# Projecting the memory keys by token, as the values are, in a hybrid decoder block on one core

## The chip, the cores and the metric

The kernel runs on one core of one Trainium2 chip. The metric is the device time of one execution in microseconds (us). Three runs of the kernel before the change are shown, and one more execution was profiled.

## What is computed

One layer of a decoder trunk with three groups of heads, and a final RMSNorm. The sequence has 1024 tokens of 2048 features, the memory 256 tokens. The change lies in group C, cross-attention into the memory: the memory is normalised per token, projected to keys and values by one matrix of 2 x 512 columns, and each of the 1024 queries attends over the 256 keys in 4 heads of 128.

```python
  h = RMSNorm(x)
  P = h @ W_in                       # one input projection for all groups
  # group A: chunked gMLP gating; group B: gated DeltaNet, 8 heads
  m = rmsnorm(mem, mem_norm_g)       # 256 x 2048
  mk, mv = split(m @ w_mem_kv)       # 256 x 512 each, 4 heads x 128
  scores = einsum('bshd,bmhd->bhsm', cq, mk) * 128 ** -0.5
  out_c = softmax(scores) @ mv * silu(c_z)
  x = x + concat(A, B, C) @ W_out
y = RMSNorm(x)
```

## The kernel before

**Arithmetic.** Every large product is made of three matmuls in fp32r: each operand is split into a high and a low part (`split_to`: a copy that rounds on ACT, then a subtraction on DVE), and `triple` issues high x high, high x low and low x high into one PSUM bank. The products of x with W_in and with W_out are arranged as seven products instead of eight, with sums and differences of blocks.

**Order.** The code doesn't issue instructions as it reads. It records them in a `Plan`; `Plan.issue` then simulates all engines with a price for each instruction and each transfer, takes at every moment the ready instruction of the smallest rank and the earliest place in the code, and so writes out a fixed order for each engine's queue. Ranks are given by `rank(...)`; matmuls of products have rank 9, so work with a smaller rank goes between them as soon as it is planned to be ready. On the chip each engine follows its order and waits for what isn't there.

**Memory projection (the first 70 us).** Sixteen steps `k`, one for each 128 of the 2048 features. A step loads 128 rows of the 2 x 512 columns of `w_mem_kv`, scales them by the norm's weights (`gcol`) and splits them into `hi` and `lo`. The memory itself is transposed once (`spread_mem`) into `mh` and `ml`, features on partitions and tokens in columns. Values are accumulated by token: the memory (128 features x 128 tokens) is the stationary operand and the 512 columns of the weights move, into two banks `va[0]`, `va[1]`, which are the first two of the four `dn` banks. Keys are accumulated by feature: 128 columns of the weights, one head, are stationary and the 256 tokens move, into the first 256 columns of the four `acc` banks (`ka`). That form leaves keys with features on partitions, as the scores need them. Since the memory's norm factor belongs to a token, for the values it is a factor for each partition, but for the keys one for each column: at step 7 the two factor columns `rm` are put on a diagonal (`dg`), a product with ones spreads them to all partitions, and ACT copies the result to `rmb`.

Between the steps, `prep` normalises, transposes and splits the first token tiles of x, in two spare `dn` banks. For the first two token tiles (`tt < H0`) the products for the decays (`decay_rows`) go into columns 256 to 383 of `acc[0]` and `acc[1]` (`first_ab`), and ACT copies them out into `sums0`.

After the last step DVE multiplies each head's keys by `rmb` into halves of the two `et` tiles, ACT scales the values, and POOL stores both to DRAM (`kv_d`). The first product of the main part (`first_product(2, ...)`) follows on TensorE in six banks, the four `acc` and the first two `dn`.

**Attention.** Near the end of the scans of group B, POOL reads keys and values back, two heads at a time, into tiles of the rings `gt` (keys) and `inv` (values); a split gives `mkT` and `mv`. `attend` then works on one head at a time with banks from the ring of the four `dn` banks (`dnr()` gives the next). The scans of group B use the first two of the same banks (`scan_banks`) and `work` the others.

Of the kernel before, what the change touches and what calls it, by code (L numbers as in the profile page):

```python
# [9 lines left out]
F32 = mybir.dt.float32  # L10
F32R = mybir.dt.float32r
AF = mybir.ActivationFunctionType
ALU = mybir.AluOpType
# [4 lines left out]
P = 128  # L18
D = 2048
KT = D // P  # L20
# [4 lines left out]
NMEM = 256  # L25
GW, DW, XW = 512, 1024, 512
NG, NH, NX = 4, 8, 4
# [33 lines left out]
class Plan:  # L61
# [27 lines left out]
    @contextmanager  # L89
    def rank(self, cls):  # L90
        old, self.cls = self.cls, cls
        yield
        self.cls = old

    @contextmanager
    def behind(self, op):
        old, self.gate = self.gate, op
        yield
        self.gate = old
# [204 lines left out]
def kernel(  # L304
# [21 lines left out]
    x, mem, w_in, out = x[0], mem[0], w_in[0], out[0]  # L326
# [7 lines left out]
    V, S, G, PE, Q = R.dve, R.act, R.pool, R.pe, R.sp  # L334
    rank, behind = R.rank, R.behind

    def C(shape, name, dt=F32):
        return sb.tile(list(shape), dt, name=name, tag=name)[:]

    def DT(shape, name, dt=F32):  # L340
        return dr.tile(list(shape), dt, name=name, tag=name)[:]
# [41 lines left out]
    def tok(ap):  # L383

        return ap.rearrange("p (t c) -> p t c", c=P)
# [14 lines left out]
    et = [C([P, HT], f"et{i}") for i in range(2)]  # L400
    ring = {t: Slots(t, 2, [P, HT]) for t in ("kT", "qT", "vs", "kd", "ai")}
# [10 lines left out]
    rm = [rms[:, i : i + 1] for i in range(2)]  # L412
# [5 lines left out]
    dnr = Ring("dn", 4, [P, HT], pool=ps)  # L418
# [6 lines left out]
    ident, ones, utri = (C([P, P], n) for n in ("ident", "ones", "utri"))  # L425
# [11 lines left out]
    def split_to(hi, lo, src, eng):  # L437
        S.copy(hi, src)
        eng.tensor_tensor(out=lo, in0=src, in1=hi, op=ALU.subtract)

    def mm(a, lhs, rhs, start, stop, cls=9):
        with rank(cls):
            return PE.matmul(a, lhs, rhs, start=start, stop=stop, skip_group_check=True)

    def triple(a, l, r, start, stop, cls=9):

        mm(a, l[0], r[0], start, False, cls)
        mm(a, l[0], r[1], False, False, cls)
        return mm(a, l[1], r[0], False, stop, cls)
# [31 lines left out]
    def rows_of(d, q, tt):  # L481
        return d[2 * q : 2 * q + 2, :, tt * 2 * P : (tt + 1) * 2 * P].rearrange("j p n -> p j n")

    def twos_of(t):
        return t.rearrange("p (j n) -> p j n", j=2)
# [11 lines left out]
    def kv_parts(k):  # L497
        n = XW if k == 0 else 2 * XW
        return [slice(i, i + n) for i in range(0, 2 * XW, n)]

    def load_kv(k):
        for i, sl in enumerate(kv_parts(k)[::-1]):
            (S if (k, i) == (0, 0) else Q).dma_start(kvraw[k % 4][:, sl], w_mem_kv[k * P : (k + 1) * P, sl])
# [22 lines left out]
    va, ka = dnr.bufs[0:2], acc  # L526
    flip = dnr.bufs[2:4]

    def spare():
        turn["dn"] = 1 - turn["dn"]  # L530
        return flip[turn["dn"]]
# [8 lines left out]
    pt = acc[3]  # L540
# [4 lines left out]
    def times_g(o, tp, q):  # L545
        V.tensor_tensor(out=o, in0=tp, in1=bc(gcol[:, 16 + 4 * q : 20 + 4 * q], P), op=ALU.mult)

    def spread_mem(q):
        h, l = (ring[t](F32R).rearrange("p (k n) -> p k n", k=4) for t in ("gt", "inv"))
        for mt in range(2):  # L550
            tp = spare()
            for k in range(4):
                PE.transpose(tp[:, k * P : (k + 1) * P], mem_rows[mt][q][:, k * P : (k + 1) * P], ident)
            sl = slice(mt * P, (mt + 1) * P)
            with rank(2):
                split_to(h[:, :, sl], l[:, :, sl], tok(tp), V)
        return h, l
# [15 lines left out]
    H0 = NT // 2  # L573

    def first_ab(tt):
        return ka[tt][:, NMEM : NMEM + P]

    def decay_rows(a, q, t, start):

        with R.together():  # L580
            for j in range(4):
                k = 4 * q + j
                PE.matmul(a[j * 32 : (j + 1) * 32], abw[:, k * 16 : k * 16 + 32], t[:, j],
                          start=start, stop=q == NQ - 1, skip_group_check=True)

    def put0(tt):
        def put(q, tp):
            t = tok(ring["tn"]())
            with rank(1):
                times_g(t, tp, q)  # L590
            with rank(2):
                split_to(ahq[q][:, tt], alq[q][:, tt], t, V)
            if tt < H0:
                decay_rows(first_ab(tt), q, t, False)
            with rank(5):
                Q.dma_start(rows_of(h0_d, q, tt), twos_of(t.rearrange("p k c -> p (k c)")))

        return put
# [8 lines left out]
    for k in range(KT):  # L607
        mh, ml = mhl[k // 4]
        if k >= 4:
            with rank(3):  # L610
                load_kv(k)
        hi, lo = kvhi[k % 2], kvlo[k % 2]
        with rank(2):
            for sl in kv_parts(k)[::-1]:
                raw = kvraw[k % 4][:, sl]
                if k == 0:
                    V.tensor_scalar(hi[:, sl], raw, gcol[:, k : k + 1], None, op0=ALU.mult)
                else:
                    S.activation(hi[:, sl], raw, AF.Copy, scale=gcol[:, k : k + 1])
                V.scalar_tensor_tensor(lo[:, sl], raw, gcol[:, k : k + 1], hi[:, sl], op0=ALU.mult, op1=ALU.subtract)  # L620
        kk = k % 4
        for mt in range(2):
            sl = slice(mt * P, (mt + 1) * P)
            triple(va[mt], (mh[:, kk, sl], ml[:, kk, sl]), (hi[:, XW:], lo[:, XW:]), k == 0, k == KT - 1)
        for h in range(NX):
            sl = slice(h * P, (h + 1) * P)
            triple(ka[h][:, :NMEM], (hi[:, sl], lo[:, sl]), (mh[:, kk], ml[:, kk]), k == 0, False)
        kvmark.append(R.ops[-1])
        if k == 0:
            with behind(kvmark[-1]), rank(2):  # L630
                G.dma_start(abw[:, 0 : KT * 16].rearrange("p (k c) -> p k c", c=16),
                            w_in[:, C_AB : C_AB + 16].rearrange("(k p) c -> p k c", p=P))
        if k in (1, 4, 8):
            with behind(kvmark[-1]):
                mhl.append(spread_mem(len(mhl)))
        if k == 1:
            load_x(0, "vs", kvmark[1:2] * 4)
        if k == 3:
            for mt in range(2):
                V.tensor_copy(rm[mt], row_scale(mem_rows[mt]))  # L640
        if k == 4:
            load_x(1, "kd", kvmark[4:5] * 4)
        if k == 5:
            prep(0, put0(0), spare)
        if k == 7:

            dg, rmb = (ring["E"]()[:, 0:NMEM] for _ in range(2))
            for mt in range(2):
                V.tensor_scalar(dg[:, mt * P : (mt + 1) * P], ident, rm[mt], None, op0=ALU.mult)
            pt = spare()  # L650
            PE.matmul(pt[:, 0:NMEM], ones, dg, start=True, stop=True)
            S.copy(rmb, pt[:, 0:NMEM])
        if k == 9:
            prep(1, put0(1), spare)
            load_x(2, "kT", (kvmark[6], kvmark[7], kvmark[7], kvmark[8]))
        if k == 13:
            load_x(3, "qT", (kvmark[10], kvmark[11], kvmark[11], kvmark[12]))
            with rank(2):
                prep(2, put0(2), spare, (2, 3, 0, 1))

    kv_d = DT([2, NX, P, NMEM], "kvd")
    with rank(1):
        kfs = [t[:, i * NMEM : (i + 1) * NMEM] for t in et for i in range(2)]
        for h in range(NX):
            V.tensor_tensor(out=kfs[h], in0=ka[h][:, :NMEM], in1=rmb, op=ALU.mult)
    for h in range(NX):
        with rank(2.5):
            G.dma_start(kv_d[0, h], kfs[h])
    for mt in range(2):
        t = ring[("ai", "kd")[mt]]()  # L670
        with rank(1):
            S.activation(t, va[mt], AF.Copy, scale=rm[mt])
        with rank(2.5):
            G.dma_start(kv_d[1, :, :, mt * P : (mt + 1) * P].rearrange("h p e -> p h e"), tok(t))
    with rank(2):
        prep(3, put0(3), spare, (2, 3, 0, 1))
    sums0 = ring["xr"].bufs[1][:, 0:HT]
# [15 lines left out]
    with rank(3.5):  # L693
        S.activation(nal, nal, AF.Exp)
        V.tensor_scalar(nal, nal, -1.0, None, op0=ALU.mult)
        pt = dnr.bufs[3]
# [1029 lines left out]
    for n, (tag, to) in enumerate((("gt", mkT), ("inv", mv))):  # L1726
        for i in range(NX // 2):
            t = ring[tag](F32R).rearrange("p (h s m) -> p h s m", h=2, s=2)
            G.dma_start(t[:, :, 1].bitcast(F32), kv_d[n, 2 * i : 2 * i + 2].rearrange("h p m -> p h m"))
            with rank(1.5):  # L1730
                split_to(t[:, :, 0], t[:, :, 1], t[:, :, 1].bitcast(F32), V)
            to += [t[:, 0], t[:, 1]]
    xab = [heir(b, f"xa{i}", f"ut{i}", 2 * HT, F32R) for i, b in enumerate(ring["ut"].bufs)]
    xat = [t[:, i * HT : (i + 1) * HT] for t in xab for i in range(2)]
# [186 lines left out]
```

## Time and profile before

| | |
|---|---|
| runs before | 1587.89, 1590.94, 1589.88 us; median 1589.88 |
| the profiled execution | 1590.5 us; its span from the first to the last instruction 1588.7 us |
| granted TensorE clock, mean | 0.998 |
| TensorE (PE) busy | 1575.6 us, 99% of the span |
| VectorE (DVE), ScalarE (ACT), GpSimd (POOL) busy | 1287.4, 1016.2, 311.7 us |
| moved by DMA | 425.77 MB, mean 268 GB/s |

Nearly all instructions are issued from one line (300, where the plan issues them), so rows of the profile are told apart by tile names: `dn<-wlo,gt` writes a `dn` bank from the tiles wlo and gt. In the memory projection `gt` and `inv` hold the memory's high and low parts (`mh`, `ml`), `whi` and `wlo` the weights' (`hi`, `lo`). In rows of the timeline the first number is the start, the second the duration (of all that are merged, with their count behind x), and brackets give the idle time of the engine before it. PE rows are matmuls and transposes, PEld loads of the stationary operand; both overlap their neighbours, and their ends are modelled, so a pace is read from start to start.

### The profile page before, as it was taken

To read this page: it belongs to the slowest core of one execution; us is meant where nothing else is said; L and a number is where in the kernel's file an instruction comes from. 1 tells how busy PE (TensorE), PEld (TensorE's weight loads), DVE (VectorE), ACT (ScalarE), POOL (GpSimd) and SP (SyncE) were. 2 spreads that over 40 slices of the span, in tenths; PEclk is the share of its full clock that TensorE was granted. 3 is DMA by queue.
4 is the path that set the end of the run, shared out by engine and by line. 5 is a ranking of instruction groups with operands and counts; after the bars stand their busy time and mean duration, and the time that the engine had idled before them with its cause. 6 is when DMAs were issued, how large, how long until landed. Compare 5 with 4: busy or idle time off the path is not lost.

```text
span 1588.7 us, 25645 instructions
## 1 busy us (share of the span) xinstructions
PE 1575.6 (99%) x8762; PEld 1317.2 (83%) x8762; DVE 1287.4 (81%) x1961; ACT 1016.2 (64%) x2088; POOL 311.7 (20%) x513
## 2 busy tenths in 40 slices
PE   9999999999999999999999999999999999999997
PEld 8878888888888888888888888888888888888886
DVE  5868996989899998997988776777768788688775
ACT  6762685776656788866775667766566864344355
POOL 1200042332402424235343133121000000000001
PEclk9999999999999999999999999999999999999999
DMA  8988868988679868986779775798877779688646
GB/s 305 319 279 278 274 214 306 349 303 268 199 253 345 270 215 283 357 306 219 263 233 356 240 259 188 242 327 257 283 255 260 260 238 355 198 283 294 202 146 238
DMA packets 213219, 425.77 MB, mean 268 GB/s; under 512 B 23112, under 2 KB 58672, under 8 KB 213088
## 3 DMA queue, kind: packets, MB, share of 16 engines
q1 hardware_dynamic: 190464, 367.40, 68.9%
q0 software_dynamic: 21840, 55.40, 10.5%
q8 instruction: 69, 1.13, 0.3%
q10 hardware_dynamic: 784, 1.33, 0.2%
q14 instruction: 62, 0.51, 0.1%
HBM read 335.40 MB, written 88.11 MB: 267 GB/s over the span
## 4 chain that ended last, share of the span: by engine, by line
PE 98%; DMA 1%; DVE 0%; issue 0%; ACTq 0%; ACT 0%; POOLq 0%; POOL 0%; DVEq 0%
PE acc L300 69%; PE dn L300 29%; DMA wraw<-in_w_in_dram 0%; DMA wraw<-in_w_mem_kv_dram 0%; DVE alo L300 0%; DVE zl L300 0%; ACTq L300 0%; ACT y2w L300 0%; DVE tn L300 0%; DVE kd L300 0%; DVE vs L300 0%; DVE inv L300 0%; POOLq L1916 0%; POOL small L300 0%; DVE whi L300 0%
## 5 line engine op out<-in xcount | busy, mean ns | idle before, releaser
L300 PE MATMUL acc<-ahi,whi 128*128 128x512 f32 (+1 forms) x1328 | 455.6, 392 | 0.0
L300 PE MATMUL acc<-ahi,wlo 128*128 128x512 f32 (+1 forms) x904 | 355.0, 393 | 0.0
L300 PEld LDWEIGHTS acc<-ahi,whi 128*128 128x128 f32 x1328 | 247.8, 188 | 47.7
L300 ACT CAST ahi<-raws 128x1024 fp32r<-128x1024 f32 x141 | 147.9, 1049 | 86.7 <-PE dn L300 40.4
L300 PEld LDWEIGHTS acc<-ahi,wlo 128*128 128x128 f32 x904 | 170.0, 188 | 32.6 <-issue 0.2
L300 PE MATMUL acc<-alo,whi 128*128 128x512 f32 (+1 forms) x480 | 187.5, 391 | 0.0
L300 PE MATMUL acc<-ahi,zh 128*128 128x512 f32 x424 | 167.2, 394 | 0.0
L300 PE MATMUL acc<-ahi,zl 128*128 128x512 f32 x424 | 167.2, 394 | 0.0
L300 PE MATMUL acc<-alo,zh 128*128 128x512 f32 x424 | 167.1, 394 | 0.0
L300 ACT CAST whi<-wraw 128x1024 fp32r<-128x1024 f32 (+1 forms) x78 | 80.6, 1033 | 70.4 <-PE acc L300 42.8
L300 DVE TENSOR_TENSOR wlo<-wraw,whi 128x1024 fp32r<-128x1024 f32 (+1 forms) x78 | 93.6, 1200 | 25.5 <-ACT whi L300 22.0
L300 POOL TENSOR_TENSOR small<-small,mhalf 128x1 f32<-128x1 f32 x26 | 16.6, 643 | 491.1 <-DVE small L300 488.9
L300 DVE TENSOR_TENSOR alo<-raws,ahi 128x1024 fp32r<-128x1024 f32 x71 | 87.5, 1233 | 21.9 <-ACT ahi L300 21.7
L300 PEld LDWEIGHTS acc<-alo,whi 128*128 128x128 f32 x480 | 90.3, 188 | 17.4
L300 DVE TENSOR_TENSOR ahi<-raws,ahi 128x1024 fp32r<-128x1024 f32 x70 | 85.4, 1220 | 18.8 <-ACT ahi L300 17.3
L300 DVE TENSOR_TENSOR alo<-y,ahi 128x1024 fp32r<-128x1024 f32 x65 | 79.3, 1220 | 17.4 <-ACT ahi L300 17.1
L300 PEld LDWEIGHTS acc<-ahi,zl 128*128 128x128 f32 x424 | 79.7, 188 | 15.3
L300 PEld LDWEIGHTS acc<-ahi,zh 128*128 128x128 f32 x424 | 79.8, 188 | 15.3
L300 PEld LDWEIGHTS acc<-alo,zh 128*128 128x128 f32 x424 | 79.7, 188 | 15.2
L300 ACT CAST ahi<-y 128x1024 fp32r<-128x1024 f32 x65 | 68.2, 1049 | 37.3 <-PE dn L300 17.6
L300 PE MATMUL dn<-whi,ahi 128*128 128x512 f32 x232 | 77.6, 389 | 0.0
L300 PE MATMUL acc<-whi,ahi 128*128 128x512 f32 x216 | 73.6, 392 | 0.0
(582 smaller groups left out, 3744.8 us busy)
## 6 DMA issues: line engine op xcount, KB each, us to landing
wraw<-in_w_in_dram SPq DMA_DIRECT2D x80, 512.0 KB, 5.1
raws<-sa SPq DMA_DIRECT2D x61, 512.0 KB, 5.3
y<-in_w_in_dram SPq DMA_DIRECT2D x40, 512.0 KB, 5.2
wraw<-in_w_out_dram SPq DMA_DIRECT2D x32, 512.0 KB, 4.9
raws<-h0d SPq DMA_DIRECT2D x29, 512.0 KB, 6.0
y<-sa SPq DMA_DIRECT2D x27, 512.0 KB, 4.8
raws<-sd SPq DMA_DIRECT2D x42, 256.0 KB, 2.9
raws<-hTd SPq DMA_DIRECT2D x16, 512.0 KB, 5.2
```

Of the source, the lines that this page charges most:

```text
L300: o.fn(*o.args, **o.kw)
```

## The change

Keys are now accumulated like the values: the memory is stationary, the 512 key columns of the weights move, and `acc[0]`, `acc[1]` take the two token tiles. The decay products of the first two token tiles move to `acc[2]`, `acc[3]`, and their first matmul starts the bank's sum. The norm factor is then one for each partition, so the diagonal, its product and the copy at step 7 go, and DVE scales two tiles of 128 x 512 in place of four of 128 x 256. POOL stores them to `key_d` in two transfers, by token. Where attention begins the keys are read back by token, 256 columns (two heads) at a time, four transposes turn them in a `dn` bank, and the split reads that bank.

```diff
     def first_ab(tt):
-        return ka[tt][:, NMEM : NMEM + P]
+        return ka[2 + tt][:, 0:P]
...
             if tt < H0:
-                decay_rows(first_ab(tt), q, t, False)
+                decay_rows(first_ab(tt), q, t, q == 0)
...
-        for h in range(NX):
-            sl = slice(h * P, (h + 1) * P)
-            triple(ka[h][:, :NMEM], (hi[:, sl], lo[:, sl]), (mh[:, kk], ml[:, kk]), k == 0, False)
+        for mt in range(2):
+            sl = slice(mt * P, (mt + 1) * P)
+            triple(ka[mt], (mh[:, kk, sl], ml[:, kk, sl]), (hi[:, 0:XW], lo[:, 0:XW]), k == 0, k == KT - 1)
...
-        if k == 7:
-
-            dg, rmb = (ring["E"]()[:, 0:NMEM] for _ in range(2))
-            for mt in range(2):
-                V.tensor_scalar(dg[:, mt * P : (mt + 1) * P], ident, rm[mt], None, op0=ALU.mult)
-            pt = spare()
-            PE.matmul(pt[:, 0:NMEM], ones, dg, start=True, stop=True)
-            S.copy(rmb, pt[:, 0:NMEM])
...
-    kv_d = DT([2, NX, P, NMEM], "kvd")
-    with rank(1):
-        kfs = [t[:, i * NMEM : (i + 1) * NMEM] for t in et for i in range(2)]
-        for h in range(NX):
-            V.tensor_tensor(out=kfs[h], in0=ka[h][:, :NMEM], in1=rmb, op=ALU.mult)
-    for h in range(NX):
+    kv_d = DT([NX, P, NMEM], "kvd")
+    key_d = DT([2, P, XW], "keyd")
+    for mt in range(2):
+        with rank(1):
+            V.tensor_scalar(et[mt], ka[mt], rm[mt], None, op0=ALU.mult)
         with rank(2.5):
-            G.dma_start(kv_d[0, h], kfs[h])
+            G.dma_start(key_d[mt], et[mt])
...
             t = ring[tag](F32R).rearrange("p (h s m) -> p h s m", h=2, s=2)
-            G.dma_start(t[:, :, 1].bitcast(F32), kv_d[n, 2 * i : 2 * i + 2].rearrange("h p m -> p h m"))
+            raw = t[:, :, 1].bitcast(F32)
+            if n == 0:
+                G.dma_start(raw, key_d[:, :, i * NMEM : (i + 1) * NMEM].rearrange("t p c -> p t c"))
+                d = dnr()
+                with rank(1.5):
+                    for h in range(2):
+                        for m in range(2):
+                            PE.transpose(d[:, (2 * h + m) * P : (2 * h + m + 1) * P], raw[:, m, h * P : (h + 1) * P], ident)
+                src = d.rearrange("p (h m) -> p h m", h=2)
+            else:
+                G.dma_start(raw, kv_d[2 * i : 2 * i + 2].rearrange("h p m -> p h m"))
+                src = raw
             with rank(1.5):
-                split_to(t[:, :, 0], t[:, :, 1], t[:, :, 1].bitcast(F32), V)
+                split_to(t[:, :, 0], t[:, :, 1], src, V)
```

More of the change, by code (lines that the diff above doesn't have):

```diff
@@ L673 @@
         with rank(2.5):
-            G.dma_start(kv_d[1, :, :, mt * P : (mt + 1) * P].rearrange("h p e -> p h e"), tok(t))
+            G.dma_start(kv_d[:, :, mt * P : (mt + 1) * P].rearrange("h p e -> p h e"), tok(t))
     with rank(2):
```

## The prediction

> **What bounds the kernel now.** I read the page first (busy times and the chain that ended last), then what TensorE waited for, then stretches of its timeline where the change cuts.
>
> ```profile
> span 1588.7 us, 25645 instructions
> ## 1 busy us (share of the span) xinstructions
> PE 1575.6 (99%) x8762; PEld 1317.2 (83%) x8762; DVE 1287.4 (81%) x1961; ACT 1016.2 (64%) x2088; POOL 311.7 (20%) x513
> ...
> PE 98%; DMA 1%; DVE 0%; issue 0%; ACTq 0%; ACT 0%; POOLq 0%; POOL 0%; DVEq 0%
> ```
>
> TensorE is busy over 99% of the span, and the chain that ended last is 98% TensorE. That alone could mislead, since matmuls overlap; so the next view is what TensorE sat idle for between 14 us and 1575 us:
>
> ```profile
> engine line waited for: us in total, times, longest us
> PE dn L300 <- DVE ai L300: 0.6, 1, 0.6
> PE dn L300 <- DVE tn L300: 0.3, 1, 0.3
> PE dn L300 <- DVE inv L300: 0.2, 1, 0.2
> ```
>
> That is 1.1 us in 1561. So the kernel is one unbroken stream of TensorE instructions, and a change pays by what it adds to or takes out of that stream, at the distance from one start to the next, not at the duration of one. Work on DVE, ACT, POOL or a queue pays only if it makes this stream wait.
>
> **The change part by part.** (1) *Key matmuls.* Before, each of the 16 k steps has 12 key matmuls that move 256 columns; after, 6 that move 512, in the form that the values have already. So one step's keys will take what its values take today. The trace has both beside each other (stretches of TensorE alone; 18.96, 28.35 start key runs, 20.40, 29.78 value runs, the last row is the spread of the factors):
>
> ```profile
> core 0: us, PE busy (x), PEclk, DMA share, GB/s
> 18.96:20.40 1.44, 1.44 (x14) 1.00 0.81 239
> 20.40:21.80 1.40, 1.40 (x9) 1.00 0.76 262
> 28.35:29.78 1.43, 1.43 (x13) 1.00 1.05 371
> 29.78:31.16 1.38, 1.38 (x8) 1.00 1.04 410
> 38.85:39.48 0.63, 0.63 (x6) 1.00 0.82 307
> ```
>
> (The counts take in neighbours that overlap an edge.) Twelve of 256 take 1.44 and 1.43 us, six of 512 take 1.40 and 1.38: 0.04 to 0.05 us less a step, 10 ns for each instruction saved at most. In the first step and a half TensorE runs slower:
>
> ```profile
> 8.86 0.84 PE L300 MATMUL acc<-gt,whi 128*128 128x256 f32 x3
> 9.50 1.05 PE L300 MATMUL dn<-ones 128*128 128x128 f32 x4
> ...
> 11.85 0.63 PE L300 MATMUL dn<-whi,inv 128*128 128x512 f32 x1
> 12.27 0.63 PE L300 MATMUL dn<-wlo,gt 128*128 128x512 f32 x1
> ```
>
> Three of 256 take 0.64 us (9.50 less 8.86), 0.213 each; one of 512 takes 0.42 (12.27 less 11.85): twice, so nothing is saved there. That leaves 14.5 steps x 0.045 = 0.65 us saved. Bounds: 0 if the pace of the columns alone counts, 14.5 x 0.06 = 0.9 if the largest pair (1.44 against 1.38) holds throughout. I take -0.65.
>
> (2) *No spread of token factors.* The two DVE products with the identity, one plain float32 matmul (two instructions), and one ACT copy go. On TensorE it is the stretch 38.85 to 39.48 above: 0.63 us. It stands among other plain float32 matmuls (the decay products), so no change of precision goes with it: -0.63, bounds -0.5 and -0.7. The DVE and ACT parts were under the stream and give nothing.
>
> (3) *Scaling and storing.* Four DVE products from PSUM become two per-partition scalings of 128x512, and four POOL DMA issues become two.
>
> ```profile
> L300 DVE TENSOR_TENSOR et<-acc,E x4: 424/425/426, 67.9 to 68.9; 128x256 f32<-128x256 f32 x4
> L300 POOL DMA_DIRECT2D kvd<-et x4: 540/544/552, 69.6 to 71.2; - x4
> ```
>
> Two DVE instructions on 128x512 should cost 0.69 each (the row of that size, the split of mkT, is quoted below), 1.4 us against 4 x 0.425 = 1.7: nothing. The first product after the keys starts at six banks; the banks of the keys are now two, not four, and come free 0.7 us after their last matmul. The cover is the work on the other four banks: acc2 and acc3 hold only the decay sums, which ACT copies out early,
>
> ```profile
> L300 ACT COPY xr<-acc x2: 242/254/266, 40.0 to 57.5; 128x128 f32<-128x128 f32 x2
> ```
>
> at 40.0 and 57.5 us, ten us before the keys end, and the two value banks are emptied under the key matmuls. Four free banks hold 4 x 3 x 3 matmuls of 256 columns at 0.12 us (1.44/12), 4.3 us of cover. If it failed, TensorE would wait 0.7 us or so, once. POOL gets 2 x 0.54 us back. Behind the stores stands the root of the fourth token tile:
>
> ```profile
> 72.39 0.99 POOL L300 TENSOR_TENSOR small<-small,mhalf 128x1 f32<-128x1 f32 x1
> ```
>
> It can run 1.1 us sooner, and the 0.3 us wait of TensorE for DVE tn (above) hangs on that tile: -0.3 to 0, I take -0.2, nearer to the wait.
>
> (4) *Eight transposes where attention begins.* The keys now come back by token; 2 x 4 plain float32 transposes turn them, into the first two dn banks. Those are the banks of the scan, and in the order of the code the transposes come after its last use, the transposes of the last heads at 1165.94. That stretch is also the price:
>
> ```profile
> 1165.94 1.03 PE L300 MATMUL dn<-ident,vs 128*128 128x128 f32 x8
> 1166.73 0.48 PE L300 MATMUL acc<-alo,zh 128*128 128x512 f32 x1
> 1167.04 0.40 PE L300 MATMUL acc<-ahi,zl 128*128 128x512 f32 x1
> ```
>
> Eight transposes take 0.79 us (1166.73 less 1165.94), and the first fp32r matmul behind them 0.31 instead of 0.23 (1.38/6): 0.08 for the change of precision. Together +0.87, or +0.95 in two blocks. I take +0.9. The Trainium skill, "TensorE: Matmul & The Clock Gate", Part 4: PE-mode transpose, gives about 275 ns for one 128x128 transpose inside a kernel; eight would be an estimated 2.2 us by it and the whole sum +0.7 instead of -0.6. The trace disagrees: the spacing above is 0.10 us. Either sum is within 0.2%.
>
> The transposes wait for the DMA that reads the keys back and for the bank:
>
> ```profile
> L300 POOL DMA_DIRECT2D gt<-kvd x2: 722/742/763, 1026.6 to 1084.0; - x2
> ...
> DMA to landing us min/median/max: 4.1/7.0/7.3
> ```
>
> The second is issued at 1084.0 and landed by 1092 at the longest; the bank comes free near 1168. So the bank is last, and neither DMA nor POOL can hold TensorE there. Behind a transpose on TensorE's queue stands all the rest, so a late bank would be paid in full; ACT's two reads of those banks are all that stands between.
>
> What moves: the split of the keys (ACT 0.62, then DVE 0.69, twice) was done at 1034 and 1092,
>
> ```profile
> L300 ACT CAST gt<-gt x2: 612/618/623, 1034.1 to 1092.5; 128x512 fp32r<-128x512 f32 x2
> L300 DVE TENSOR_TENSOR gt<-gt x2: 679/685/691, 1034.9 to 1093.1; 128x512 fp32r<-128x512 f32 x2
> ```
>
> and goes to about 1169. Their first reader starts at 1198.3,
>
> ```profile
> L300 PE MATMUL dn<-gt,xa x90: 274/282/367, 1198.3 to 1292.1; 128*128 128x256 f32 x90
> ```
>
> 29 us later. ACT and DVE have a hole right there:
>
> ```profile
> 1172.69 1.05 ACT L300 CAST whi<-wraw 128x1024 fp32r<-128x1024 f32 x1 [2.97 <-PE acc L300]
> 1173.78 1.22 DVE L300 TENSOR_TENSOR wlo<-wraw,whi 128x1024 fp32r<-128x1024 f32 x1 [2.61 <-ACT whi L300]
> ```
>
> 2.97 us of idle ACT before 1172.69 hold the 1.24 us of both ACT halves, and 2.61 us of idle DVE before 1173.78 its 1.38. So: nothing. If the hole were gone, the splits would push the weights' splits back by 2.6 us at most (2 x (0.62 + 0.69)). Two more calls of the dn ring shift the banks of attention by two of four; all four are idle by then: nothing.
>
> **Sum.** -0.65 - 0.63 - 0.2 + 0.9 = -0.6 us (-0.58). The profiled execution took 1590.5 us (its span 1588.7), 0.6 above the median of the runs, 1589.88; from the median I forecast **1589.3 us**. A measurement of this kernel tells about 0.2% (3.2 us; the three runs lie 3.05 apart), so this is no change.
>
> **The rivals.** *Slower: the weights come late behind the moved splits.* After 1165 the transfers are near their limit:
>
> ```profile
> core 0: us, PE busy (x) PEld busy (x) DVE busy (x) ACT busy (x) POOL busy (x), PEclk, DMA share, GB/s
> 1165.00:1175.00 10.00, 10.00 (x50) 8.35 (x49) 6.36 (x8) 5.46 (x7) 0.00 (x0) 1.00 0.95 295
> 1175.00:1198.00 23.00, 23.00 (x103) 19.06 (x102) 19.09 (x21) 11.31 (x15) 0.00 (x0) 1.00 0.93 316
> ```
>
> The weights are loaded into slots that ACT and DVE free by their splits. If the 2.6 us of key splits delay one slot so that its load loses its place,
>
> ```profile
> wraw<-in_w_in_dram SPq DMA_DIRECT2D x80, 512.0 KB, 5.1
> ```
>
> TensorE waits up to one such landing, 5.1 us: -0.6 + 5.1 = +4.5, 1594.4 us. It decides from a wait of 3.8 us (3.2 + 0.6). For it: DMA shares of 0.95 and 0.93, and DVE busy 19.09 of 23. Against: TensorE is busy 23.00 of 23.00, ACT under half. Chance 0.14.
>
> *Faster: weight loads bind the narrow matmuls.* If each matmul waited for its own weight load, 96 loads fewer would give 96 x 0.198,
>
> ```profile
> L300 PEld LDWEIGHTS acc<-gt,whi 128*128 128x128 f32 x64 | 12.5, 198 | 0.9 <-issue 0.2
> ```
>
> 19.0 us: 1570.9. Against it stands the pace of 0.12 us in the key runs, shorter than one load, so loads already overlap. The Trainium skill, "Perfetto Trace Analysis", Identifying the Most-Contended Engine, would judge TensorE's headroom by the busy share of the weight loads rather than of matmuls, and speaks for this rival; the pace in the trace speaks against. Chance 0.03.
>
> *Faster by the order behind it.* Every start after 67 us is planned anew. Each block of plain float32 work that joins another saves 0.08 us, so 33 of them would be needed ((3.2 - 0.6)/0.08); a smaller saving lies inside the forecast. 1586.6 at that point. Chance 0.08.
>
> *The transposes do not overlap.* From the 1.03 us of the eight, seven spacings of 0.10 leave 0.33 for one; end to end they take 2.6 instead of 0.8, the sum is +1.2 and the time 1591.1, still no change. Against it: the eight at 1165.94. Chance 0.04.
>
> **How the numbers follow.** The forecast has 0.71; with the dear transposes, 0.75 within 0.2%. Faster by more: 0.03 + 0.08 = 0.11. Slower by more: 0.14. The range reaches to the slower rival's 1594.4 and, below, past the re-planned order, 1585.5: it leaves out the weight-load rival and the tail of the other, with the scatter of a median (1.5 to either side) inside.
>
> **What would show it.** Right: key runs of 6 at 1.38 to 1.40 us; no matmul at 38.9 with E; eight transposes near 1168 with 0.10 us between starts; the sum of TensorE's waits still near 1 us. Wrong: a wait of TensorE for wlo, zl or a weight transfer between 1168 and 1198, an idle TensorE near 68 us while DVE scales keys, or a difference beyond 3 us spread thinly over the whole span, which would be the new order.

## The result and the profile after

| kernel | median, us | runs | ratio to the kernel before, 95% |
|---|---|---|---|
| before | 1589.09 | 6, 1587.89 to 1590.94 | |
| changed | **1596.05** | 6, 1593.12 to 1598.16 | 1.0042 (1.0032 to 1.0053) |
| changed, a second set beside other runs | 1593.59 | 7, 1591.54 to 1597.17 | 1.0033 (1.0021 to 1.0044) |

The change is 0.3 to 0.4% slower, 5 to 7 us, where no change was forecast. The changed kernel also scatters over 6.6 us. The kernel before, run beside each set below, took 1588.3 to 1589.2 us, so the ratios compare sets better than differences of their medians do. The profiled run took 1595.31 us (span 1593.6), 4.8 above the profiled run before. Its page, in the lines that answer to those of before, and the chain that ended last:

```profile
span 1593.6 us, 25450 instructions
PE 1575.3 (99%) x8672; PEld 1312.0 (82%) x8672; DVE 1285.7 (81%) x1957; ACT 1016.0 (64%) x2087; POOL 304.1 (19%) x511
...
PE 91%; DMA 5%; DVE 2%; issue 1%; POOL 0%; ACT 0%; SPq 0%; ACTq 0%; POOLq 0%; DVEq 0%
```

TensorE's busy time is 0.3 us less than the 1575.6 before, with 90 instructions less. That does not prove the sum over instructions right: the busy time grows where the clock falls, and the kernel of experiment 8, with the same 8762 TensorE instructions as before, was busy for 1573.1 us. The chain has 91% TensorE in place of 98%, with 5% DMA; that is no measure of the loss either, for experiment 8, as fast as the kernel before, has 91% too. The waits say more. What TensorE waited for between 14 and 1575 us (before: three waits, 1.1 us):

```profile
PE acc L300 <- ACT ahi L300: 2.2, 1, 2.2
PE dn L300 <- DVE kT L300: 1.4, 1, 1.4
PE dn L300 <- DVE qTw L300: 1.0, 2, 0.7
PE dn L300 <- DVE tn L300: 0.3, 1, 0.3
PE dn L300 <- ACT kd L300: 0.3, 1, 0.3
PE dn L300 <- DVE inv L300: 0.2, 1, 0.2
```

That is 5.4 us. Stretches of TensorE where the keys end and the first product begins, before:

```profile
core 0: us, PE busy (x), PEclk, DMA share, GB/s
67.00:75.00 8.00, 8.00 (x68) 1.00 1.05 397
75.00:80.00 5.00, 4.65 (x39) 1.00 1.04 390
```

and after:

```profile
67.00:75.00 8.00, 5.72 (x44) 1.00 0.98 340
75.00:80.00 5.00, 3.68 (x20) 0.66 1.06 394
```

TensorE does 107 instructions there before and 64 after, and from 75 to 80 us it has 0.66 of its clock. Matched one by one (the n-th TensorE instruction of a kind in both traces), the changed kernel stands 1.35 us ahead at 17 us, 1.8 ahead at 70 us, and 3.2 behind at 156: 5.0 lost. The lead at 17 us is scatter of the start and no gain of the change: three profiles with the old keys (experiments 4, 8 and SLACK 630 in 10) are 1.2 to 1.3 ahead there, and a second profile of the changed kernel is 0.6 behind. It loses 1.6 more at 292 us (the wait for DVE kT), gains 0.9 at 620 (a wait of before that is gone) and loses 0.96 between 1160 and 1180, at the transposes. Together +4.9.

**What ends the wait near 76 us.** Two queues in series. ACT in the changed kernel, with the idle time before an instruction and its releaser in brackets:

```profile
74.61 1.06 ACT L300 ACTIVATE jk<-ut 128x1024 bf16<-128x1024 f32 x1 [1.35 <-DMA ut<-in_x_dram]
75.58 0.19 ACT L300 ACTIVATION_READ_ACCUMULATOR jk<-ut 128x1 f32 x1
75.67 0.60 ACT L300 CAST ahi<-tn 128x512 fp32r<-128x512 f32 x1
```

and TensorE:

```profile
71.43 0.66 PE L300 MATMUL dn<-ident,qTw 128*128 128x128 f32 x4 [0.68 <-DVE qTw L300]
72.42 0.66 PE L300 MATMUL dn<-ident,qTw 128*128 128x128 f32 x4 [0.34 <-DVE qTw L300]
73.42 0.66 PE L300 MATMUL dn<-ident,qT 128*128 128x128 f32 x4 [0.34 <-DVE tn L300]
76.32 0.58 PE L300 MATMUL acc<-ahi,inv 128*128 128x256 f32 x1 [2.25 <-ACT ahi L300]
```

A square of the sixth token tile (`jk<-ut`) waits on ACT for its load; the cast of the fourth tile's first quarter stands behind it; TensorE waits for the cast. Before the change the same square did not wait:

```profile
73.99 1.06 ACT L300 ACTIVATE jk<-ut 128x1024 bf16<-128x1024 f32 x1
```

The last part of that load left SP at 68.05 before and at 66.67 after, so it was not issued late; it took 5.5 us to land before (at 73.54) and 7.8 after. A second difference stands earlier, on SP. (Tiles are counted from 0 as in the code, `tt`: the sixth is tile 5, the fourth tile 3.) Stores of the normalised quarters before:

```profile
49.41 0.38 SPq L300 DMA_DIRECT2D h0d<-tn  x1
50.39 3.02 SPq L300 DMA_DIRECT2D h0d<-tn  x2
61.35 1.86 SPq L300 DMA_DIRECT2D h0d<-tn  x3
```

and after:

```profile
50.16 0.38 SPq L300 DMA_DIRECT2D h0d<-tn  x1
58.62 2.65 SPq L300 DMA_DIRECT2D h0d<-tn  x4
```

The second store of tile 1 leaves SP at 58.6 in place of 50.4, behind bulk loads. A buffer of the ring `tn` is written again only when its store is done, so tile 2 is prepared later, and tile 3 after it: its transposes, at 71.4, stand where TensorE has nothing else ready. The theory to test was that this late store is the loss; the rivals were the transposes and the form of the keys themselves, and the new order as a whole.

### The profile page after: what moved, and what is told of

Read it like the earlier page. It is cut to its first block, busy times and chain, and to the rows that moved or that the text cites. A ratio compares the mean times of both kernels' runs of the same rounds, so it can differ in the third digit from the quotient of the medians.

```text
span 1593.6 us, 25450 instructions
## 1 busy us (share of the span) xinstructions
PE 1575.3 (99%) x8672; PEld 1312.0 (82%) x8672; DVE 1285.7 (81%) x1957; ACT 1016.0 (64%) x2087; POOL 304.1 (19%) x511
## 3 DMA queue, kind: packets, MB, share of 16 engines
q8 instruction: 68, 1.11, 0.3%
## 4 chain that ended last, share of the span: by engine, by line
PE 91%; DMA 5%; DVE 2%; issue 1%; POOL 0%; ACT 0%; SPq 0%; ACTq 0%; POOLq 0%; DVEq 0%
PE acc L300 64%; PE dn L300 27%; DMA wraw<-in_w_in_dram 1%; DMA inv<-in_w_in_dram 1%; DMA ut<-in_x_dram 0%; DMA aiw<-in_w_in_dram 0%; DMA vsw<-in_x_dram 0%; DMA h0d<-tn 0%; DVE wlo L300 0%; DMA qTw<-sa 0%; DMA wraw<-in_w_mem_kv_dram 0%; DVE kT L300 0%; DMA qT<-in_x_dram 0%; DVE alo L300 0%; DMA y<-in_w_in_dram 0%
```

## The experiments

**1. The store first.** In `put0` of the changed kernel:

```diff
-            with rank(5):
+            with rank(2.7 if tt in (1, 2) else 5):
                 Q.dma_start(rows_of(h0_d, q, tt), ...)
```

> The changed kernel, with one edit: the stores of the normalised quarters of token tiles 1 and 2 (h0d<-tn) get rank 2.7 in place of 5, so SP issues them ahead of the bulk loads that wait beside them. Theory (late store): in the changed kernel the store of the second tn quarter of tile 1 left SP at 58.6 us in place of 50.4, the next tile's quarters could not be written into tn, tile 2 was prepared under the first product in place of under the keys, and TensorE ran out of operands between 71.4 and 76.3 us (3.6 us of gaps), then at part of its clock to 80 us. It expects that store near 51 us, the waits of TensorE for DVE qTw and ACT ahi at 71 to 77 us mostly gone, and 4 to 5 us back: 1591.0 to 1592.5 us, ratio to the kernel before 1.001 to 1.002. Rival (keys by token and the transposes cost it themselves): unchanged, 1596, ratio 1.004. Rival (the plan's order as a whole, no one place): a wait elsewhere takes its place, 1594 to 1598.

1589.99 us, ratio 1.0011 (1.0002 to 1.0020), a little better than the theory's range: 6.1 us below the first set of the changed kernel and 3.6 below the second, with keys by token and all eight transposes in place. The store left at 51.2, and the stretch is full:

```profile
67.00:75.00 8.00, 8.00 (x66) 1.00 1.05 397
75.00:80.00 5.00, 4.94 (x42) 1.00 1.04 384
```

So keys by token and transposes do not cost 5 us by themselves. That the store's lateness was the cause, and not merely that this order is another one, is not shown by this run alone.

**2. No transposes, twice, and the changed kernel again.** `src = raw`, without the `PE.transpose` calls.

> The changed kernel without the eight transposes where attention begins; the split reads the stored keys as they lie, so group C's scores are made of untransposed keys. Theory (late store): the eight transposes cost 1.0 us (the same instructions stood 4.0 us later than before ahead of them and 5.0 behind), so 1595.0 us, and the wait at 71 to 77 us stays. Rival (transposes and moved splits are the loss): 5 us or more back, 1590 to 1591. Rival (they cost nothing, the offset is something else): 1596.

1591.45 us, ratio 1.0014 (1.0006 to 1.0023): not the 1.0 us below that the theory gave, but 4.6, near the rival. Its profile has no offset between 1160 and 1180, and so agrees with 1.0 for the transposes; but it was ahead by 2.7 us at 80 us already, where both kernels have the same order. There the square of `ut` did not wait, TensorE waited 0.93 for the cast instead of 2.25, and the clock stayed up. The changed kernel and this one, each once more:

> The changed kernel once more, beside the next run on one chip. Up to 1160 us it has the same order on every engine as the kernel without transposes (1591.45 in the first set), yet the two differed by 4.6 us and their profiles by 2.7 us at 80 us already: there ACT waited 1.35 us for the load of an x tile (ut) in the one and not in the other, and the clock fell in the one and not in the other. Theory (late store, with an outcome that varies from run to run by when that load lands): this run falls between, 1592 to 1596, and stays 1 us above the next. Rival (the transposes cost 4.6 by something not yet seen): 1596, and 4 to 5 above the next.

> The kernel without transposes once more, on the chip of the run above; scores of group C are again made of untransposed keys. Theory: 1 us below that run. Rival: 4 to 5 us below it.

1593.59 with the transposes and 1591.52 without, 2.1 apart, between the two forecasts. In the traces the matched offset grows by 0.96 us between 1160 and 1180 in the two profiles of the changed kernel and in those of experiments 1, 3, 6, 7 and 9, which all have the transposes, and by 0 in both without. That part is settled. In both profiles with transposes the load of `ut` came late (1.35 and 1.11 us of waiting ACT), in both without it came in time (it took 7.8 and 7.7 us to land with them, 6.8 and 6.2 without). Up to 1038 us, and not 1160 as the expectation has it, all engines have the same order in the two kernels, so nothing in their orders explains it; why the load was slow is open.

**3. Keys by token in halves of 256 columns.**

```diff
-            triple(ka[mt], ..., (hi[:, 0:XW], lo[:, 0:XW]), k == 0, k == KT - 1)
+            for c in (slice(0, NMEM), slice(NMEM, XW)):
+                triple(ka[mt][:, c], ..., (hi[:, c], lo[:, c]), k == 0 and c.start == 0, k == KT - 1)
```

> The changed kernel with the keys still by token but moved in halves of 256 columns (12 matmuls a step, as before the change). If width is worth what the profiles show (a run of 12 at 1.43 to 1.44 us, a run of 6 at 1.38 to 1.40), the keys end 0.5 to 0.65 us later. Theory (late store): the time goes by what the new order does to the store and tile 2 and not by width; with the same late store 1596.5, and if the store leaves early again in this order, 1592 to 1593. Rival (512 columns hold the low part's consumer back, since each matmul needs the whole 512 of wlo): 256 columns give back over 3 us without any move of the store.

1593.77 us, ratio 1.0030 (1.0019 to 1.0040). A key run of 12 took 1.44 (19.96 to 21.40), one of 6 in the changed kernel 1.40:

```profile
20.42 0.40 PE L300 MATMUL acc<-whi,gt 128*128 128x512 f32 x1
...
21.82 0.40 PE L300 MATMUL dn<-whi,gt 128*128 128x512 f32 x1
```

The width is worth 0.04 us a step. The first two stores of tile 1 left SP early here, at 49.2 and 51.0 (the third only at 59.9), and yet the time, above the 1592 to 1593 expected for an early store, was that of the changed kernel: a first sign against the late store as the one cause.

**4. The kernel before, with the late store put into it.** The stores of tile 1's second to fourth quarters are recorded behind the keys of step 12.

> The kernel before, with one edit: the stores of the second to fourth tn quarters of token tile 1 are held until the keys of step 12 are done, about where the changed kernel issued them. Nothing else of the change is in it. Theory (late store): the preparation of tile 2 slips by some 10 us, TensorE waits 3 to 5 us between 67 and 80 us or a little later, the clock falls for one stretch behind it, and the time is 1593 to 1595 us, ratio 1.003 to 1.004, with none of the change in it. Rival (the store is a companion of the loss, not its cause): within 1 us of the kernel before, 1588 to 1590.

1599.50 us, ratio 1.0071 (1.0059 to 1.0084): ten us lost by an edit that moves three stores and has nothing of the change. But the place was wrong. SP issued them at 58.8, and TensorE was busy 8.00 of 8.00 and 5.00 of 5.00 us in the two stretches; it waited later:

```profile
163.59 0.79 PE L300 MATMUL acc<-ahi,whi 128*128 128x512 f32 x1 [4.64 <-ACT whi L300]
173.13 0.50 PE L300 MATMUL acc<-ahi,whi 128*128 128x512 f32 x1 [2.31 <-ACT whi L300]
```

From 161.65 us TensorE also had half its clock for 6.83 us, in which it was busy for 4.89. All its waits are 8.3 us in place of 1.1; with some 2.4 us for the half clock that is about the ten. How the held stores made `whi` late was not followed up.

**5. The kernel before, with the store first.** Rank 2.7 for all `h0d` stores.

> The kernel before with the stores of all h0d<-tn at rank 2.7 in place of 5, and nothing of the change. In it those stores are not late (second store of tile 1 at 50.4 us). Theory (late store): nothing to gain, within 1 us of the kernel before, 1588 to 1590. Rival (an earlier store is a gain of its own, whatever the form of the keys, so the store run of the changed kernel is no evidence on the change): 3 us or more faster, 1586 or less.

1593.94 us, ratio 1.0035 (1.0022 to 1.0047): slower by as much as the change, which neither forecast allowed. The store isn't the cause by itself: stores that go first push loads back on the same queue. The last part of the load of `ut` left SP at 69.83, 1.8 us later than before, and took 7.3 us to land in place of 5.5. ACT:

```profile
77.20 1.06 ACT L300 ACTIVATE jk<-ut 128x1024 bf16<-128x1024 f32 x1 [3.09 <-DMA ut<-in_x_dram]
78.16 0.19 ACT L300 ACTIVATION_READ_ACCUMULATOR jk<-ut 128x1 f32 x1
78.26 1.13 ACT L300 CAST ahi<-tn 128x512 fp32r<-128x512 f32 x2
```

That is the link of the changed kernel again, without the change: the square waits for the load, the cast for the square, and TensorE 1.2 us for the cast. The theory became: a load lands late, in part by SP's order, and ACT's order lets the late load reach TensorE.

**6. Store and order of the terms.** The changed kernel with tile 1's store at rank 2.7, and in each key bank high x high, low x high, high x low.

> The changed kernel with the store of token tile 1 at rank 2.7 (tile 2's left at 5), and with the three key matmuls of a bank in the order high x high, low x high, high x low, so that the one that needs wlo comes last. Theory (late store): as the first store run, 1589 to 1591; the other order takes at most the wait for wlo in the first step, near 10 us, 0.3 to 0.5 us. If keys by token at 512 columns save what the profiles show (0.5 for the width, 0.6 for the spread, less 1.0 for the transposes) and every wait is gone, 1589.0 is the best it can give, no change against the kernel before. Rival (order as a whole): 1593 or more, by a wait elsewhere.

1591.48 us, ratio 1.0021 (1.0012 to 1.0031), between theory and rival; again a square of `ut` waited, 2.93 us, and TensorE 1.1 for the cast behind it.

**7. The cast ahead of the square.** The edit is aimed at ACT's link alone: the preparation of the sixth tile may start behind the cast of the fourth tile's first quarter (`casts` collects them in `put0`).

```diff
         for i in range(NT):
-            prep1(i)
+            with behind(casts[-4] if i == 1 else R.gate):
+                prep1(i)
```

> The changed kernel, with one edit: the preparation of the sixth token tile (its squares jk<-ut on ACT) may start only behind the ACT cast of the first quarter of the fourth tile (ahi<-tn). In the changed kernel that cast stood on ACT behind a square of ut, which waited 1.35 and 1.11 us (two profiles) for the load of ut, and TensorE waited 2.2 and 2.0 us for the cast. Theory now (two queues in series: SP's order decides when the tiles' store and the later x loads land, ACT's order puts a cast that TensorE needs behind a square that needs such a load): the wait for ACT ahi near 76 us goes or falls under 1 us, the clock holds to 80 us, 2 to 3 us back of the changed kernel's 1593.6, 1590.5 to 1592. Rival (the store alone): no change, 1593 to 1596. Rival (the order as a whole): another wait takes its place, 1593 or more.

1591.88 us, ratio 1.0018 (1.0010 to 1.0027), 1.7 us below the second set of the changed kernel, 4.2 below the first (0.15 and 0.24% by the ratios). The cast now goes ahead:

```profile
73.37 0.62 ACT L300 CAST ahi<-tn 128x512 fp32r<-128x512 f32 x1 [1.32 <-DVE tn L300]
73.89 1.05 ACT L300 ACTIVATE jk<-ut 128x1024 bf16<-128x1024 f32 x1
```

Matched one by one, this profile gains 3.4 us on the first profile of the changed kernel between 70 and 82 us and 3.1 on the second, and gives back 2.3 and 0.9 by 200 us, in an order that differs from 72 us on. The wait for ACT ahi is gone from the list, and the clock held:

```profile
PE dn L300 <- DVE qTw L300: 1.0, 2, 0.7
PE dn L300 <- DVE tn L300: 0.9, 2, 0.6
PE acc L300 <- ACT whi L300: 0.6, 2, 0.3
PE dn L300 <- DVE ai L300: 0.4, 1, 0.4
PE dn L300 <- ACT kd L300: 0.3, 1, 0.3
```

The store still left late (58.4), and the waits for `qTw` that come with late tiles are still there.

**8. The same cure for the kernel before with the store first** (here for the sixth and all later tiles).

> The kernel before with the stores at rank 2.7 as in the run that gave 1593.94, and the same edit of the squares behind the cast. In that run a square of ut waited 3.09 us on ACT for its load, with the cast behind it, and TensorE waited 1.16 us for the cast. Theory (two queues in series): the price of the early store was paid through that link, so it goes: 1588 to 1590.5. Rival (the early store costs elsewhere, on SP or the DMA): still 1593 to 1594.

1589.24 us, ratio 1.0000 (0.9991 to 1.0009): 4.7 us back, all that the early store had cost. SP's order is that of experiment 5 until 98 us and the load was slow again (8.2 us), but no TensorE instruction waited behind it. So the link is shown to cost time; that it was the whole price is not. The two profiles differ by 2.6 us: 1.3 at 17 us already, where nothing differs but the start, then 2.0 between 70 and 156 us, and 0.6 the other way later. The profiled run of experiment 5 was the fastest of its five, so what its slower ones paid for is in no trace; and behind the link ACT's order is another one up to 233 us. TensorE's waits:

```profile
PE dn L300 <- DVE ai L300: 1.4, 1, 1.4
PE dn L300 <- DVE tn L300: 0.3, 1, 0.3
```

**9. The changed kernel with all three edits** (tile 1's store, terms, cast for the sixth and later tiles).

> The changed kernel with three edits: the store of tile 1 at rank 2.7, the matmul that needs wlo last in each bank, the squares of the sixth tile behind the cast. The same without the last edit gave 1591.48, with a wait of 1.1 us for ACT ahi behind a square that waited 2.93 us for ut. Theory: 1 to 2 us below that, 1589.5 to 1590.5. By the terms of the instructions (width 0.5 and spread 0.6 saved, transposes 1.0 added) 1588.2 to 1589 is the floor, so it does not beat the kernel before. Rival (order as a whole): 1591 or more.

1590.16 us, ratio 1.0004 (0.9996 to 1.0013): no change against the kernel before, and no gain. None of the versions beats the kernel before.

**10. The same work in another order.** Four kernels with no change in their work, two of each form, only in one constant of the planner, so that the same instructions are ordered anew.

```diff
-    SLACK = 600.0
+    SLACK = 630.0
```

> The kernel before with nothing changed in its work: only the planner's constant SLACK is 630 in place of 600, so that the same instructions come in another order from some point on. Rival theory (any new order loses against this one, whatever the change says): 1591 to 1594, slower by about as much as the change. Theory (the loss is made by the places named): within 1.5 us of the kernel before unless one of them appears in its trace too (the second store of tile 1 later than 55 us, a cast of ahi behind a late ut).

> The kernel before with its work unchanged; the planner's constant DMA_FIXED is 2800 in place of 2900, which gives another order. With SLACK changed it gave 1591.46, 2.3 us slower. If any order but this one loses (the kernel before stands in a lucky order): 1591 to 1596 again. If only the two named places lose: 1588 to 1590, unless its trace shows the second store of tile 1 after 55 us or a cast of ahi behind a late ut.

> The changed kernel with its work unchanged and SLACK 630 in place of 600. By the terms of the instructions alone every order of it should stand near 1589 to 1590 where TensorE has no wait. If the loss belongs to one order: away from 1593.6, by 1 us at least, most likely down to 1590 to 1592, with the waits of TensorE in its trace accounting for what is above 1590. If it belongs to the change: 1593 to 1596.

> The changed kernel with its work unchanged and DMA_FIXED 3000 in place of 2900, one more order. The same two forecasts: 1590 to 1592.5 with the excess in waits named by its trace if the loss is the order's, 1593 to 1596 if it is the change's.

| work of | order | us | ratio, 95% |
|---|---|---|---|
| before | SLACK 630 | 1591.46 | 1.0017 (1.0009 to 1.0026) |
| before | DMA_FIXED 2800 | 1600.59 | 1.0076 (1.0061 to 1.0091) |
| changed | SLACK 630 | 1597.51 | 1.0059 (1.0042 to 1.0076) |
| changed | DMA_FIXED 3000 | 1593.11 | 1.0027 (1.0017 to 1.0037) |

A correction of 3 to 5% in a constant that no instruction sees moved the kernel before by 2.3 and 11.8 us, more than the change did. In the slowest, two waits of the kind of experiment 4 stand first, at the same place (161.7 and 170.2 us), with half the clock for 3.41 us behind the second:

```profile
PE acc L300 <- ACT whi L300: 5.7, 2, 4.1
PE dn L300 <- ACT vs L300: 1.5, 1, 1.5
PE dn L300 <- ACT y2w L300: 1.4, 1, 1.4
```

Its store left late too (59.6), but no square of `ut` waited between 70 and 80 us. In the kernel before with SLACK 630 neither of the two named places appears; there 1.7 us of waiting for ACT vs stands at 742 us. That one, 2.3 us above the kernel before where the theory allowed 1.5, is what decides; the slowest has the late store that its expectation excepted. So the named places are two of several, and the rival of the whole order holds in this form: *most* new orders meet some such place. Experiments 8 and 9 (1.0000 and 1.0004) show orders that lose nothing measurable.

Of the changed kernel's two orders the first lies above both forecasts, and the second, 1593.11, just inside the range that was to mean that the loss is the change's. With no other edit, three orders of the old work took 1589, 1591.5 and 1600.6, three of the changed work 1593.1, 1593.6 to 1596.1 and 1597.5. They overlap, and three are too few to tell whether the change also shifts its spread.

## Why the prediction was wrong

**The failed step.** The sum took TensorE's waits over as they were, "still near 1 us": for the waits of a new order it had nothing, and gave no reason. "Every start after 67 us is planned anew" stood in the prediction, but only as a rival on the fast side, with 0.08, priced at 0.08 us for each joined block; the last of the signs of being wrong names the new order, "spread thinly over the whole span", with no price. What the runs showed in its place: 5.4 us of waits instead of 1.1, 3.6 of them between 71 and 77 us, and half the clock for 3.41 us behind those, so the loss stood in a few places. Four other orders of the work of before (experiments 4, 5 and 10) took 1591.5 to 1600.6, and only the one with the cast's link cut came back to 1589.2; six further orders of the changed work took 1590.0 to 1597.5. The kernel before stands at the good end of the six orders of its work that were run, and an edit that makes the planner begin again draws from such a spread. The order had begun to differ long before 67 us, with the store at 50 us.

**Why the profile misled.** 1.1 us of waits in 1561 was read as robust: "work on DVE, ACT, POOL or a queue pays only if it makes this stream wait". The sentence is right, and it was not turned round: in that stretch the DMA share was 1.04 to 1.05 (the table of before above), a load and a store shared SP, and the cover of the casts was never measured. The load of the square of `ut` that ran at 73.99 without a wait had landed 0.45 us before it.

**The slower rival** had the mechanism half right (a load that loses its place in a queue reaches TensorE through ACT) and the place wrong: it was set between 1165 and 1198, where TensorE after the change does not wait at all, so that its 1594.4 lies near the measured times is luck:

```profile
1165.00:1250.00 85.00, 85.00 (x418) 1.00 0.82 272
```

**The terms.** (1) Keys: 1.44 to 1.40, so 0.04 x 14.5 = 0.58 against 0.65. (2) The spread's stretch is gone. TensorE's busy time fell by 0.3 us, where (1), (2) and (4) add up to -0.38; by what is said above on the busy time, that they agree is luck. In experiment 9 the matched offset between 17 and 156 us is 0.6 us of gain, where (1) to (3) promised 1.5; what ate the rest was not separated. From 17 us to the end it is 1.0 of loss, and the medians are 1.0 apart too, where the sum promised 0.6 of gain. (3) The four banks covered the scaling as forecast, since no wait in the list names `et` (the two scalings took 0.75 us each against 0.69); but the wait for DVE tn that POOL's relief was to shorten is still 0.3 us, so that -0.2 is 0. (4) Transposes: +0.96 against +0.9. They run in two blocks, the second of them

```profile
1174.27 0.60 PE L300 MATMUL dn<-ident,gt 128*128 128x128 f32 x4
1174.62 0.48 PE L300 MATMUL acc<-ahi,wlo 128*128 128x512 f32 x1
1174.93 0.63 PE L300 MATMUL acc<-ahi,whi 128*128 128x512 f32 x2
```

0.35 us for four and 0.31 for the matmul behind, as the row at 1165.94 had said. The Trainium skill, "TensorE: Matmul & The Clock Gate", Part 4: PE-mode transpose, gives about 275 ns for one, and the prediction read the trace as against it. But that figure is a duration, and the trace agrees with it: one of these eight lasts 0.27 us. They overlap, with 0.11 us from start to start, so the estimate of 2.2 for eight laid end to end was the prediction's own step. The keys' late split held nobody. By its own terms the change is worth about nothing, and 1590.0 to 1590.2 in its best orders (ratios 1.0011 and 1.0004) is that, or up to 0.2% slower.

## What to carry to other kernels

Where an order is planned from prices and then fixed, an edit has two effects: what its instructions cost, and a new draw of the order. Before an edit of less than one per cent is credited or blamed, run the same work under two or three null edits of the planner; their spread is the measure (here two such edits cost the kernel before 2.3 and 11.8 us). Where a wait of the bound engine is seen, follow it through every queue it crosses: here a cast that needed no load stood behind a square that did, and with the cast ahead the median was 4.7 us lower in one kernel and 1.7 to 4.2 in the other, of which the traces show 2 and 3 at that place.

## What was not expected of the hardware

**The clock can fall after a short, broken idle stretch.** After the stretch from 70.8 to 76.3 us, in which only twelve transposes ran and the longest gap was 2.25 us, matmuls of 256 columns started 0.21 us apart instead of 0.12:

```profile
77.99 0.41 PE L300 MATMUL acc<-ahi,whi 128*128 128x256 f32 x1
78.20 0.41 PE L300 MATMUL acc<-alo,whi 128*128 128x256 f32 x1
78.41 0.41 PE L300 MATMUL acc<-ahi,wlo 128*128 128x256 f32 x1
```

The granted clock was half for 3.41 us, and full on both sides:

```profile
75.83:79.24 3.41, 2.92 (x13) 0.50 1.06 392
```

That is where some 1.4 of the 5.0 us went (5.0 less 3.6 us of gaps from 71 to 77). In the second profile of the changed kernel, in the repeat of experiment 2 and, twice, in the slowest kernel of experiment 10 the half clock lasted 3.41 us too, in experiment 4 twice that, 6.83. Whether it falls varies: with the same order and the same four gaps (0.68, 0.34, 0.34, 0.93 us) one run without transposes had the full clock from 75 to 80 us and its repeat 0.66. In the first of them:

```profile
75.00:80.00 5.00, 5.00 (x42) 1.00 1.07 382
```

and in the repeat:

```profile
75.00:80.00 5.00, 5.00 (x32) 0.66 1.07 381
```

The Trainium skill, "TensorE: Matmul & The Clock Gate", Part 1: The HAM clock gate (the "warmup" mystery), has a free-running window of about 3.4 us after which an idle TensorE drops to half its clock, and its Part 4 says that transposes do not count as busy in the same way. Both agree with these rows (5.5 and some 4.2 us of nothing but transposes and gaps, a pace of about half for 3.41 us or twice that, an outcome that varies from run to run); no run here separates the two. Transposes and gaps are not enough by themselves: experiment 3 had 3.8 us of nothing else from 70.2 to 74.0 us, experiment 5 3.6 from 75.3 to 78.9, and the clock stayed full in both.
